# Splitting the second group's router logits load at row 126, as the first group's already is

## The chip, the cores and the metric

The kernel runs on one core of one Trainium2 chip. The metric is the device time of one execution, in microseconds (us); for a kernel that is timed it is the median of several runs. A profile is one more execution, recorded by the hardware profiler; its span runs from its first instruction to its last.

## The reference: top-2 gating and a scaled copy

There are 16 x 1024 = 16384 tokens. Each has 512 floats of `x` and 8 router logits. The output holds each token's 512 floats twice, each copy scaled by one of two weights:

```python
probs = softmax(router_logits)                     # over 8 experts
topk_indices = np.argsort(probs, axis=-1)[..., -2:]
topk_probs = np.take_along_axis(probs, topk_indices, axis=-1)
topk_probs = topk_probs / np.sum(topk_probs, axis=-1, keepdims=True)
out = (x[:, :, None, :].repeat(2, axis=2) * topk_probs[..., None])
```

Normalised over the two best experts, the softmax is a sigmoid of the difference of the two largest logits, so the kernel needs only that difference. The input is 33.6 MB of `x` and 0.5 MB of logits, the output 67.1 MB, in float32 throughout.

## The kernel before, in words

The 128 partitions of SBUF hold tokens. `GROUPS = [65, 63]` (line 42) cuts the tokens into two groups: in the first each partition holds 65 consecutive tokens, in the second 63. So one partition's logits are a run of 65 x 8 x 4 = 2080 bytes of memory for the first group and of 63 x 8 x 4 = 2016 bytes for the second. These runs are called rows below; a transfer of logits moves up to 128 of them, one for each partition.

All loads and all stores but one are issued by SyncE (SP), in program order; the first store is issued by ScalarE (ACT). `keep_in_program_order` holds the order as written, so SP's list is fixed: a load of 2 tokens and one of 4 tokens for each partition (line 122), then the logits (the `if` at line 128), then loads of 28 and 31 tokens, which ends the first group's input. The logits come in three transfers: the first group's rows 0 to 125, its rows 126 and 127 (both line 133), and the second group's 128 rows in one (line 136). Behind them stand the first group's stores (line 156), each waiting for VectorE, then the second group's three loads (16, 16 and 31 tokens), which wait until the first group's buffers have been stored, then the second group's stores. An `x` load of 28 tokens moves 28 x 2048 = 57344 bytes for each partition, one of 31 tokens 63488; a store of 15 tokens moves 61440 (two copies of each token), one of 16 tokens 65536. At the very end an empty SP instruction (line 160) waits for all but the last transfer.

`top2_weights` (line 14) takes all logits of both groups at once: VectorE (DVE) finds the largest and second largest of 8 by a tree of max and min over both groups' 128 tokens for each partition. Its first instruction (line 26) therefore waits for all logits transfers. Line 36 takes the difference, ACT makes the two weights (lines 37 and 38). Then DVE multiplies (line 143): `x` rows times the two weights, into the buffer `osp` or in place into `xs`, and each product is stored. The logits lie in `osp` too, in a part of it that later products overwrite.

The framework gives every transfer one of eight completion semaphores, in turn. A transfer that is given a semaphore which an earlier transfer has used waits, where it isn't already known to be done, until that earlier one has landed.

Of the kernel before, what the change touches and what calls it, by code (L numbers as in the profile page):

```python
# [1 line left out]

# [4 lines left out]

F32 = mybir.dt.float32
ALU = mybir.AluOpType
ACTF = mybir.ActivationFunctionType  # L10
P = 128


def top2_weights(nc, WA, dlt, room, logits, E):

    tt = nc.vector.tensor_tensor
    hi, lo, n = None, None, E  # L20
    while n > 1:
        n //= 2
        if hi is None:
            a, b = logits[:, :, 0:n], logits[:, :, n : 2 * n]
            nhi, nlo = room(n), b
            tt(nhi, a, b, op=ALU.max)  # L26
            tt(nlo, a, b, op=ALU.min)  # L27
        else:
            a, b = hi[:, :, 0:n], hi[:, :, n : 2 * n]
            nhi, nlo, tmp = room(n), room(n), room(n)  # L30
            tt(tmp, lo[:, :, 0:n], lo[:, :, n : 2 * n], op=ALU.max)  # L31
            tt(nlo, a, b, op=ALU.min)  # L32
            tt(nlo, nlo, tmp, op=ALU.max)  # L33
            tt(nhi, a, b, op=ALU.max)  # L34
        hi, lo = nhi, nlo
    tt(dlt, hi[:, :, 0], lo[:, :, 0], op=ALU.subtract)  # L36
    nc.scalar.activation(WA[:, :, 0], dlt, ACTF.Sigmoid, scale=-1.0)  # L37
    return nc.scalar.activation(WA[:, :, 1], dlt, ACTF.Sigmoid, scale=1.0)  # L38

GROUPS = [65, 63]

LOADS = [[2, 4, 28, 31], [16, 16, 31]]
BASE = [0, 1]

STORES = [
    [(0, 3, "osp", 0), (3, 15, "osp", 3), (18, 16, "xs", 0), (34, 15, "osp", 0), (49, 16, "xs", 33)],
    [(0, 16, "osp", 2), (16, 16, "xs", 0), (32, 15, "osp", 0), (47, 16, "xs", 32)],
]  # L50

L = 18

FREE = [3, 2]


@with_exitstack
def kernel(
    ctx: ExitStack,
    tc: tile.TileContext,  # L60
    x: bass.AP,
    router_logits: bass.AP,
    k: bass.AP,
    out: bass.AP,
):
    nc = tc.nc
    B, S, D = x.shape
    E = router_logits.shape[-1]
    N = B * S
    assert int(k) == 2 and E == 8 and N == P * sum(GROUPS)  # L70
    M = N // P

    x_v, o_v, rl_v = [], [], []
    t0 = 0
    for n in GROUPS:
        t1 = t0 + P * n
        x_v.append(
            x.rearrange("b s d -> (b s) d")[t0:t1].rearrange("(p m) d -> p m d", p=P)
        )
        o_v.append(  # L80
            out.rearrange("b s k d -> (b s) k d")[t0:t1].rearrange(
                "(p m) k d -> p m k d", p=P
            )
        )
        rl_v.append(
            router_logits.rearrange("b s e -> (b s) e")[t0:t1].rearrange(
                "(p m) e -> p m e", p=P
            )
        )
        t0 = t1  # L90

    wpool = ctx.enter_context(tc.tile_pool(name="wpool", bufs=1))
    xs = wpool.tile([P, max(GROUPS), D], F32)
    osp = wpool.tile([P, L, 2, D], F32)
    WA = wpool.tile([P, M, 2], F32)
    dlt = wpool.tile([P, M], F32)


    flat = osp.rearrange("p l k d -> p (l k d)")
    taken = [0]  # L100

    def room(n):
        o = taken[0]
        taken[0] += M * n
        return flat[:, o : o + M * n].rearrange("p (m n) -> p m n", n=n)

    logits = room(E)

    def place(where, at, n):

        if where == "osp":
            return osp[:, at : at + n]
        return xs[:, at : at + 2 * n, :].rearrange("p (r k) d -> p r k d", k=2)

    moved = []
    m0 = 0
    for g, G in enumerate(GROUPS):
        x0, r = BASE[g], 0
        for n in LOADS[g]:
            moved.append(  # L120
                tc.keep_in_program_order(
                    nc.sync.dma_start(  # L122
                        xs[:, x0 + r : x0 + r + n, :], x_v[g][:, r : r + n, :]
                    )
                )
            )
            r += n
            if g == 0 and r == 6:
                n0 = GROUPS[0]
                for p0, p1 in [(0, 126), (126, P)]:  # L130
                    moved.append(
                        tc.keep_in_program_order(
                            nc.sync.dma_start(logits[p0:p1, :n0], rl_v[0][p0:p1])  # L133
                        )
                    )
                tc.keep_in_program_order(nc.sync.dma_start(logits[:, n0:], rl_v[1]))  # L136
                weights = top2_weights(nc, WA, dlt, room, logits, E)
        assert r == G
        for r, n, where, at in STORES[g]:
            og = place(where, at, n)  # L140
            again = where == "osp" and at == 0 and r > 0
            for a, b in [(0, FREE[g]), (FREE[g], n)] if again else [(0, n)]:
                product = nc.vector.tensor_tensor(  # L143
                    og[:, a:b],
                    xs[:, x0 + r + a : x0 + r + b, :]
                    .unsqueeze(2)
                    .to_broadcast([P, b - a, 2, D]),
                    WA[:, m0 + r + a : m0 + r + b, :]
                    .unsqueeze(3)
                    .to_broadcast([P, b - a, 2, D]),  # L150
                    op=ALU.mult,
                )

            queue = nc.scalar if g == r == 0 else nc.sync
            moved.append(
                tc.keep_in_program_order(queue.dma_start(o_v[g][:, r : r + n], og))  # L156
            )
        m0 += G

    seen = tc.keep_in_program_order(nc.sync.nop())  # L160
    for ins in [weights, product] + moved[:-1]:
        tc.add_manual_dep(
            seen.ins,
            ins.ins.name,
            mybir.DependencyInfo(
                mybir.DependencyClass.Sync, mybir.DependencyReason.DATA
            ),
            reason="all but the last transfer is done",
        )


# [1 line left out]
_INS = ['x', 'router_logits', 'k']  # L173
_OUTS = [((16, 1024, 2, 512), 'float32')]

_NUMBERS = {'k': 2}


# [26 lines left out]
```

## Time and profile before

| | |
|---|---|
| time, median of 3 runs (lowest to highest) | 239.89 us (239.77 to 240.0) |
| the profiled execution's own time | 239.86 us |
| its span | 238.1 us |
| DVE busy | 141.9 us, 22 instructions |
| ACT busy | 1.8 us, 3 instructions |
| data moved by the DMA engines | 101.19 MB in 2592 packets |
| HBM read, written | 34.08 MB, 67.11 MB |

The core has 16 DMA engines. A transfer issued by SP (queue q1 in the profile) or by ACT (queue q10) is cut into packets that the engines work off, each engine in order. A view of a stretch of time counts a packet, its bytes and its time in full where the packet starts, so the DMA share of a short stretch can be over 1.00 or far below it; over a long stretch 1.00 means that 16 engines were busy all the time. "us to landing" is the time from the issue of a transfer to its completion.

### The profile page before, as it was taken

To read this page: it belongs to the slowest core of one execution; us is meant where nothing else is said; L and a number is where in the kernel's file an instruction comes from. 1 tells how busy PE (TensorE), PEld (TensorE's weight loads), DVE (VectorE), ACT (ScalarE), POOL (GpSimd) and SP (SyncE) were. 2 spreads that over 40 slices of the span, in tenths; PEclk is the share of its full clock that TensorE was granted. 3 is DMA by queue.
4 is the path that set the end of the run, shared out by engine and by line. 5 is a ranking of instruction groups with operands and counts; after the bars stand their busy time and mean duration, and the time that the engine had idled before them with its cause. 6 is when DMAs were issued, how large, how long until landed. Compare 5 with 4: busy or idle time off the path is not lost.

```text
span 238.1 us, 109 instructions
## 1 busy us (share of the span) xinstructions
DVE 141.9 (60%) x22; ACT 1.8 (1%) x3; POOL 0.2 (0%) x4
## 2 busy tenths in 40 slices
DVE  0560499999789999200000699999406999960000
ACT  2000000000000000000000000000000000000000
POOL 0000000000000000000000000000000000000000
DMA  7999998989898989989899999998998989989894
GB/s 261 419 443 503 406 461 381 465 372 495 363 496 374 507 351 475 495 352 529 352 435 424 418 479 448 405 507 363 440 440 363 518 352 507 454 372 518 352 518 187
DMA packets 2592, 101.19 MB, mean 425 GB/s; under 512 B 288, under 2 KB 416, under 8 KB 672
## 3 DMA queue, kind: packets, MB, share of 16 engines
q1 hardware_dynamic: 2448, 99.62, 97.3%
q10 hardware_dynamic: 144, 1.57, 1.6%
HBM read 34.08 MB, written 67.11 MB: 425 GB/s over the span
## 4 chain that ended last, share of the span: by engine, by line
DMA 48%; DVE 40%; SPq 1%; issue 0%; DVEq 0%
DVE osp L143 25%; DMA xs<-in_x_dram 25%; DMA out_dram<-osp 22%; DVE xs L143 14%; SPq L122 0%; SPq L133 0%; SPq L136 0%; SPq L156 0%; DVEq L143 0%
## 5 line engine op out<-in xcount | busy, mean ns | idle before, releaser
L143 DVE TENSOR_TENSOR osp<-xs,WA 128x3072 f32<-128x3072 f32 (+5 forms) x7 | 69.4, 9909 | 61.0 <-DMA xs<-in_x_dram 46.8
L143 DVE TENSOR_TENSOR xs<-xs,WA 128x16384 f32<-128x16384 f32 x4 | 68.9, 17225 | 0.1
L26 DVE TENSOR_TENSOR osp<-osp 128x512 f32<-128x512 f32 x1 | 0.7, 692 | 8.8 <-DMA osp<-in_router_logits_dram 8.8
L37 ACT ACT_TABLE_LOAD x1 | 1.3, 1283 | 0.7 <-PEq L186 0.7
L27 DVE TENSOR_TENSOR osp<-osp 128x512 f32<-128x512 f32 x1 | 0.7, 691 | 0.0
L32 DVE TENSOR_TENSOR osp<-osp 128x256 f32<-128x256 f32 (+1 forms) x2 | 0.7, 352 | 0.0
L34 DVE TENSOR_TENSOR osp<-osp 128x256 f32<-128x256 f32 (+1 forms) x2 | 0.7, 352 | 0.0
L31 DVE TENSOR_TENSOR osp<-osp 128x256 f32<-128x256 f32 (+1 forms) x2 | 0.7, 351 | 0.0
L33 DVE TENSOR_TENSOR osp<-osp 128x256 f32<-128x256 f32 (+1 forms) x2 | 0.7, 350 | 0.0
L37 ACT ACTIVATE WA<-dlt 128x128 f32<-128x128 f32 x1 | 0.3, 315 | 10.7 <-DVE dlt L36 10.7
L36 DVE TENSOR_TENSOR dlt<-osp 128x128 f32<-128x128 f32 x1 | 0.3, 293 | 0.0
L38 ACT ACTIVATE WA<-dlt 128x128 f32<-128x128 f32 x1 | 0.3, 298 | 0.0
L186 POOL MEMSET const-bfloat16-1.0<- 128x1 bf16 x1 | 0.1, 101 | 0.0
L186 POOL MEMSET const-uint8-127<- 128x1 uint8 x1 | 0.1, 101 | 0.0
L186 POOL MEMSET const-float32-0.0<- 128x1 f32 x1 | 0.1, 98 | 0.2 <-issue 0.2
L186 POOL MEMSET const-float32-1.0<- 128x1 f32 x1 | 0.1, 98 | 0.0
## 6 DMA issues: line engine op xcount, KB each, us to landing
out_dram<-osp SPq DMA_DIRECT2D x3, 7680.0 KB, 23.1
xs<-in_x_dram SPq DMA_DIRECT2D x2, 7936.0 KB, 41.4
xs<-in_x_dram SPq DMA_DIRECT2D x2, 4096.0 KB, 40.2
xs<-in_x_dram SPq DMA_DIRECT2D x1, 7168.0 KB, 24.2
out_dram<-osp ACTq DMA_DIRECT2D x1, 1536.0 KB, 26.5
xs<-in_x_dram SPq DMA_DIRECT2D x1, 1024.0 KB, 5.9
xs<-in_x_dram SPq DMA_DIRECT2D x1, 512.0 KB, 3.6
osp<-in_router_logits_dram SPq DMA_DIRECT2D x1, 255.9 KB
```

The lines of the kernel that those rows point to most:

```text
L26: tt(nhi, a, b, op=ALU.max)
L27: tt(nlo, a, b, op=ALU.min)
L31: tt(tmp, lo[:, :, 0:n], lo[:, :, n : 2 * n], op=ALU.max)
L32: tt(nlo, a, b, op=ALU.min)
L33: tt(nlo, nlo, tmp, op=ALU.max)
L34: tt(nhi, a, b, op=ALU.max)
L36: tt(dlt, hi[:, :, 0], lo[:, :, 0], op=ALU.subtract)
L37: nc.scalar.activation(WA[:, :, 0], dlt, ACTF.Sigmoid, scale=-1.0)
L38: return nc.scalar.activation(WA[:, :, 1], dlt, ACTF.Sigmoid, scale=1.0)
L143: product = nc.vector.tensor_tensor(og[:, a:b], xs[:, x0 + r + a : x0 + r + b, :] .unsqueeze(2) .to_broadcast([P, b - a, 2, D]), WA[:, m0 ...
L186: nc = _bacc.Bacc("TRN2", target_bir_lowering=False, num_devices=1)
```

## The change

The second group's logits are loaded in two transfers as well, rows 0 to 125 and rows 126 and 127, by the same loop as the first group's. SP issues four logits transfers instead of three, in the same place. Both parts of the second group are now in the list `moved`, which the last SP instruction waits for. The bytes, the rows, their places in memory and in SBUF and every instruction of DVE and ACT stay as they were.

```diff
             if g == 0 and r == 6:
-                n0 = GROUPS[0]
-                for p0, p1 in [(0, 126), (126, P)]:
-                    moved.append(
-                        tc.keep_in_program_order(
-                            nc.sync.dma_start(logits[p0:p1, :n0], rl_v[0][p0:p1])
+                at = 0
+                for h, m in enumerate(GROUPS):
+                    for p0, p1 in [(0, 126), (126, P)]:
+                        moved.append(
+                            tc.keep_in_program_order(
+                                nc.sync.dma_start(
+                                    logits[p0:p1, at : at + m], rl_v[h][p0:p1]
+                                )
+                            )
                         )
-                    )
-                tc.keep_in_program_order(nc.sync.dma_start(logits[:, n0:], rl_v[1]))
+                    at += m
                 weights = top2_weights(nc, WA, dlt, room, logits, E)
```

In the built program one more thing moves: with one transfer more ahead of them, all later transfers get the next of the eight semaphores. The load of 31 tokens of the first group so comes to the semaphore of the very first load (2 tokens), and SP waits for that load's landing before it issues the 31 tokens. No other transfer's waits change but in the semaphores' numbers; DVE's first instruction and ACT's store name four logits transfers instead of three.

## The prediction

> **What bounds the kernel now.** First the page: busy times and DMA queues.
>
> ```profile
> DVE 141.9 (60%) x22; ACT 1.8 (1%) x3; POOL 0.2 (0%) x4
> ...
> DMA packets 2592, 101.19 MB, mean 425 GB/s; under 512 B 288, under 2 KB 416, under 8 KB 672
> ...
> q1 hardware_dynamic: 2448, 99.62, 97.3%
> q10 hardware_dynamic: 144, 1.57, 1.6%
> ```
>
> DVE works 60% of the span; the packets of the two queues fill 97.3 + 1.6 = 98.9% of the 16 engines' time. So the next view cuts the span by stretches: until the logits are in, and from there to the last packets (columns: stretch, length, DVE, ACT, POOL, clock, DMA share, GB/s).
>
> ```profile
> 1.70:9.40 7.70, 0.61 (x1) 0.30 (x1) 0.00 (x0) 1.00 1.08 392
> 9.40:236.30 226.90, 141.31 (x22) 0.51 (x2) 0.00 (x0) 1.00 1.00 433
> ```
>
> From 9.40 to 236.30 us the share is 1.00 at 433 GB/s: no engine ever runs dry there. The time is therefore the number of bytes that an engine must move, plus the start, plus what slows packets down. Compute is off the path. The start and the end, by counts of packets in short stretches: 233.9 to 234.4, 234.4 to 234.7, 236.3 to 236.8, 236.9 to 237.0.
>
> ```profile
> DMA packets 15, 0.98 MB, mean 1966 GB/s; under 512 B 0, under 2 KB 0, under 8 KB 0
> ...
> q1 hardware_dynamic: 15, 0.98, 453.4%
> ```
> ```profile
> DMA packets 1, 0.07 MB, mean 218 GB/s; under 512 B 0, under 2 KB 0, under 8 KB 0
> ```
> ```profile
> DMA packets 15, 0.00 MB, mean 0 GB/s; under 512 B 15, under 2 KB 15, under 8 KB 15
> ```
> ```profile
> DMA packets 1, 0.00 MB, mean 0 GB/s; under 512 B 1, under 2 KB 1, under 8 KB 1
> ```
>
> The last set of big packets is one for each engine: 15 start before 234.4, one after it. Each lasts 4.534 x 16 x 0.5 / 15 = 2.42 us for 65536 bytes, 27.1 GB/s. Each engine closes a transfer with a tiny packet: 15 before 236.8, one after 236.9. So **one engine ends last, by 0.1 us at least**, and whatever is added to its packets is added to the time. The page's 288 tiny packets show how the split works already: 19 transfers (7 loads of `x`, 3 of logits, 9 stores) on 16 engines each would leave 304; 16 fewer is what results when the 126 rows use 14 engines (9 rows each, 2 packets fewer) and the 2 rows use two engines (14 fewer).
>
> **The change part by part.**
>
> (1) *Rows by engine, the term that counts.* 128 rows on 16 engines are 8 each. Split, 14 engines carry 9 rows of 2016 bytes, two of all engines one more, and two carry none. What does one row cost? Counts of 5.88 to 6.61 us, then 6.61 to 7.65, the two stretches in which logits move:
>
> ```profile
> DMA packets 123, 0.26 MB, mean 354 GB/s; under 512 B 16, under 2 KB 24, under 8 KB 117
> ...
> q1 hardware_dynamic: 123, 0.26, 90.4%
> ```
> ```profile
> DMA packets 142, 0.36 MB, mean 349 GB/s; under 512 B 18, under 2 KB 105, under 8 KB 140
> ...
> q1 hardware_dynamic: 142, 0.36, 130.5%
> ```
>
> First stretch: 0.904 x 16 x 0.73 = 10.56 us of packet time; off come 6 packets of 8 KB (8192 bytes at 27 GB/s, 0.30 us each, 1.8) and 16 tiny ones (about 0.01 each, 0.15); 8.6 us remain for 101 rows, 0.085 us a row. Second stretch: 1.305 x 16 x 1.04 = 21.7 us; off come two big packets (57344 bytes at 27.1 GB/s, 2.1 us each at least, 4.2) and 18 tiny ones (0.2); 17.3 us for 122 rows, 0.14 us a row. So rows go at full speed first and at little over half of it from 6.61 us on: **a slow stretch** costing 122 x (0.14 - 0.085) / 16 = 0.4 us for each engine. One row more is 0.085 to 0.14 us; I take 0.11, the middle, since with the split the row ends in either stretch. For the two engines with two rows more it is 0.22, and for the two without rows 8 x 0.085 to 8 x 0.14 = 0.7 to 1.1 less. The engine that ends last is one of the 14 by 14 in 16, and of the two with 0.22 by 2 in 16. Taken: **+0.11**; bounds 0 (if the slow stretch is a limit on all rows together, spreading the same rows otherwise costs nothing) and 2 x 0.14 = +0.28.
>
> [...]
>
> (2) *One more issue on SP.* Issue times, and the queue's order:
>
> ```profile
> L133 SPq DMA_DIRECT2D osp<-in_router_logits_dram x2: 242/350/457, 1.6 to 2.1; - x2
> ```
> ```profile
> 0.72 0.85 SPq L122 DMA_DIRECT2D xs<-in_x_dram  x2
> 1.63 0.74 SPq L133 DMA_DIRECT2D osp<-in_router_logits_dram  x2
> 2.41 0.36 SPq L136 DMA_DIRECT2D osp<-in_router_logits_dram  x1
> 2.81 0.95 SPq L122 DMA_DIRECT2D xs<-in_x_dram  x2
> 8.79 0.69 DVE L26 TENSOR_TENSOR osp<-osp 128x512 f32<-128x512 f32 x1 [8.79 <-DMA osp<-in_router_logits_dram]
> ...
> 16.65 0.37 ACTq L156 DMA_DIRECT2D out_dram<-osp  x1
> ...
> 43.26 0.35 SPq L156 DMA_DIRECT2D out_dram<-osp  x1
> ```
>
> 0.46 + 0.24 instead of 0.36: the 28 tokens are issued 0.34 us later, at 3.15 instead of 2.81. The first load was issued at 0.72, and the first packets start at 1.7 (below), a lag of 1.0; so the 28 tokens are ready at about 4.2. Who asks first for them shows in the counts of 7.0 to 7.3 us:
>
> ```profile
> DMA packets 39, 0.18 MB, mean 584 GB/s; under 512 B 7, under 2 KB 35, under 8 KB 37
> ```
>
> 39 - 37 = 2 big packets, the only two up to 7.65: the two engines without first-group rows, at 7.0 at the earliest. Without their 8 second-group rows too they ask at 5.9 to 6.3. Cover 1.7 us: cost 0; without cover, 0.34.
>
> (3) *The new wait on SP.* The 31 tokens wait for the landing of the first load (512 KB). Behind it on SP stand the first group's stores, the first issued at 43.26.
>
> ```profile
> DMA  0000000000000000099991532679998989997977
> ...
> xs<-in_x_dram SPq DMA_DIRECT2D x1, 7168.0 KB, 24.2
> ...
> xs<-in_x_dram SPq DMA_DIRECT2D x1, 512.0 KB, 3.6
> ```
>
> (The first line is 0 to 4 us in slices of 0.1.) The first load lands at 0.72 to 1.10 + 3.6 = 4.3 to 4.7; the 31 tokens are issued then instead of by 3.76, and needed only when the 28 tokens run out, at about 2.81 + 24.2 = 27. Cover over 20 us: cost 0.
>
> (4) *The weights come later.* DVE's line 26 starts with the last logits landing, 8.79; two engines with two more rows put it off by up to 0.28, ACT's store from 16.65 to 16.9 and the first SP store from 43.26 to 43.5. With the lag of 1.0 that is ready at 44.5. Counts of 44 to 47 us and of 47.0 to 47.2:
>
> ```profile
> DMA packets 16, 1.02 MB, mean 339 GB/s; under 512 B 0, under 2 KB 0, under 8 KB 0
> ```
> ```profile
> DMA packets 4, 0.12 MB, mean 614 GB/s; under 512 B 2, under 2 KB 2, under 8 KB 2
> ```
>
> Up to 47 all engines move the last 63488 bytes of the 31 tokens; the first two turn to the store after 47.0. Cover 2.5 us: cost 0; if a store came later than that, each 1 us late is 1 us. Later stores give no stall either, by the share of 1.00. The two engines with no rows come up to 1.1 us earlier: cover 1.4 still.
>
> (5) *The end.* The last SP instruction names more transfers, all long landed: 0.
>
> **Sum:** 239.86 (the profiled execution) + 0.11 = 239.97. The runs' median, 239.89, is 0.03 above that execution, so the sum stands for either.
>
> [...]
>
> **The rivals.**
>
> *A: the slow stretch goes.* For: rows of the first group, in 14 engines' shares, ran at 0.085 while the second group's, in 16 shares, met the slow stretch. Against: 35 of the first group's rows stand in the slow stretch too (140 under 8 KB - 105 under 2 KB). If it goes: 239.97 - 0.4 = 239.57.
>
> *B: the last engine catches up.* Starts of the last packets but one of the second group's 31 tokens, and of the first ones of the store behind them:
>
> ```profile
> 155.30:155.50 0.20, 0.20 (x1) 0.00 (x0) 0.00 (x0) 1.00 1.46 635
> 155.50:155.94 0.44, 0.44 (x1) 0.00 (x0) 0.00 (x0) 1.00 4.33 1876
> 155.94:156.00 0.06, 0.06 (x1) 0.00 (x0) 0.00 (x0) 1.00 2.44 1058
> 160.30:160.70 0.40, 0.40 (x1) 0.00 (x0) 0.00 (x0) 1.00 5.69 2458
> 160.70:160.90 0.20, 0.20 (x1) 0.00 (x0) 0.00 (x0) 1.00 0.00 0
> 160.90:160.95 0.05, 0.05 (x1) 0.00 (x0) 0.00 (x0) 1.00 3.03 1311
> ```
>
> 2, 13 and 1 packets at 155.3 to 156.0 without a straggler; at 160 us 15 start by 160.7, one after 160.9. The lag of 0.2 that sets the end arose where loads turn to stores. With other engines ahead it may fall otherwise: 239.97 - 0.2 = 239.77. With A: 239.37.
>
> *C: the slow stretch spreads (slower).* Place: 5.9 to 8 us. The 14 engines have 18 small rows each in a line instead of 17. If all go at 0.14, that is 18 x 0.055 = 1.0 us lost instead of 0.4, so +0.6 on top of 0.11: 240.57. It decides once over two thirds of the rows are slow: 12 x 0.055 = 0.66, 0.26 more than now, with 0.22 for an engine of two more rows is 0.48. For: the engines without rows start their 28 tokens beside the others' rows sooner, and the slow stretch began when two engines were ahead. Against: those two read big packets only from 7.0, 0.4 after it began.
>
> *D: the new 2-row transfer makes its engines stop.* If they took up the next transfer only after one lag of 1.0, the two end at 239.97 + 1.0 = 240.97. Against: the first group's 2 rows stand in the same line, and rows flowed at a share of 0.90 and more. [...]
>
> **How the numbers follow.** Forecast 239.97 (239.86 to 240.14): 0.54. A alone 0.13, B alone 0.12, A with B 0.06; C 0.12; D 0.03. 0.2% is 0.48 us, about what a measurement of this kernel can tell from no change. Faster than 239.41: A with B, 0.06, and a little of A, 0.02: 0.08. Slower than 240.37: C for the most, 0.11, and D, 0.03: 0.14. Same: 0.78. The range from 239.45 to 240.4 leaves out A with B, D and nearly all of C, 0.2.
>
> **What would show it.** 288 packets under 512 B again (20 transfers, 32 fewer than 320) and 416 under 2 KB; SP's logits issues 1.4 to 1.5 us in all; line 26 at 8.8 to 9.1 us; two engines at big packets from about 6 us; a share of 1.00 from 9.4 us to the end. A slow stretch of other length shows as other time for the rows between 6 and 8 us (A, C), a last tiny packet closer to the rest as B. I'm wrong if a stretch after 9.4 us is below 1.00, or if small rows move over 0.48 us.

## The result, and the profile after

| | before | changed |
|---|---|---|
| median time, 12 runs each | 239.94 us (239.77 to 240.12) | 240.47 us (240.28 to 240.98) |
| ratio to before, 95% interval | | 1.0023 (1.0014 to 1.0032) |
| the profiled execution: time, span | 239.86, 238.1 us | 240.28, 238.5 us |

The changed kernel is slower by 0.53 us, where 0.11 was forecast; the time lies 0.07 above the range. The profiled executions are 0.42 apart.

The page of the changed kernel has the same packets, and one line that moved by a whole microsecond:

```profile
DMA packets 2592, 101.19 MB, mean 424 GB/s; under 512 B 288, under 2 KB 416, under 8 KB 672
...
L26 DVE TENSOR_TENSOR osp<-osp 128x512 f32<-128x512 f32 x1 | 0.7, 691 | 9.8 <-DMA osp<-in_router_logits_dram 9.8
```

DVE's first instruction waits for the logits until 9.8 us instead of 8.8. Its SP queue and that instruction, in order of time:

```profile
1.63 1.44 SPq L134 DMA_DIRECT2D osp<-in_router_logits_dram  x4
3.11 1.63 SPq L122 DMA_DIRECT2D xs<-in_x_dram  x2
9.83 0.69 DVE L26 TENSOR_TENSOR osp<-osp 128x512 f32<-128x512 f32 x1 [9.83 <-DMA osp<-in_router_logits_dram]
```

From the end of the first loads to the start of the 28 tokens on all engines (5.8 to 9.3 us), first the kernel before, then the changed one:

```profile
DMA packets 330, 1.52 MB, mean 435 GB/s; under 512 B 48, under 2 KB 176, under 8 KB 304
...
q1 hardware_dynamic: 330, 1.52, 119.4%
```
```profile
DMA packets 334, 1.56 MB, mean 445 GB/s; under 512 B 48, under 2 KB 176, under 8 KB 304
...
q1 hardware_dynamic: 334, 1.56, 139.9%
```

Both stretches hold the same work but for four 8 KB packets: 48 tiny packets, 128 rows of 2016 and 128 of 2080 bytes, 16 big packets (the first 57344 bytes of the 28 tokens, one for each engine), and 10 or 14 packets of 8 KB. At full speed (0.009, 0.082, 0.085, 2.116 and 0.305 us; the kernel with neither group split, below, shows that these prices add up exactly) that is 58.7 and 60.0 us of packet time. The engines took 1.194 x 16 x 3.5 = 66.9 and 1.399 x 56 = 78.3. So the **excess** is 8.2 / 16 = 0.51 us for each engine before, and 18.3 / 16 = 1.15 after. The same sum is made for each experiment below; it is the number to watch. The slow stretch of the prediction more than doubled, and it took in the big packets. The two engines without rows show that. Packets from 6.2 to 6.6 us of the changed kernel, then from 9.4 to 9.9:

```profile
DMA packets 74, 0.25 MB, mean 614 GB/s; under 512 B 9, under 2 KB 9, under 8 KB 72
```
```profile
DMA packets 2, 0.11 MB, mean 229 GB/s; under 512 B 0, under 2 KB 0, under 8 KB 0
```

74 - 72 = 2 big packets start by 6.6; these engines' second ones start only after 9.4: the packets started at 6.28 and 6.46 took 3.2 and 3.3 us instead of 2.1. Before, where they started at 7.0 to 7.3, the two second ones came between 9.4 and 9.7:

```profile
DMA packets 2, 0.11 MB, mean 382 GB/s; under 512 B 0, under 2 KB 0, under 8 KB 0
```

So the lead of 0.4 us or more was lost at once.

Not all of 0.64 us more excess reached the end. The last 57344-byte packets of the 28 tokens, before (22.5 to 24.0 us) and changed (22.5 to 25.0):

```profile
q1 hardware_dynamic: 16, 0.92, 155.6%
```
```profile
q1 hardware_dynamic: 16, 0.92, 84.6%
```

1.556 x 16 x 1.5 / 16 = 2.33 us each before, 0.846 x 2.5 = 2.12 each in the changed kernel. So before lost 0.21 us there that the changed kernel didn't lose: 0.64 - 0.21 = 0.43, and the profiled times differ by 0.42. That the two meet so closely is partly chance: the last packets of the 31 tokens took 0.06 us more in the kernel before as well (0.800 x 3.0 = 2.40 from 44 to 47 us, against 0.976 x 2.4 = 2.34 from 44 to 46.4), 14 engines of the changed kernel carry a row more (0.08 at full speed), and a mean over 16 engines isn't the engine that ends last. At the end (tiny packets from 236.0 to 236.1 and from 236.8 to 237.4 of the changed kernel) the two light engines are done 0.7 us and more ahead of the other 14:

```profile
DMA packets 2, 0.00 MB, mean 0 GB/s; under 512 B 2, under 2 KB 2, under 8 KB 2
```
```profile
DMA packets 14, 0.00 MB, mean 0 GB/s; under 512 B 14, under 2 KB 14, under 8 KB 14
```

### The profile page after: what moved, and what is told of

Same layout as the page of the kernel before. It is cut to its first block, busy times and chain, and to the rows that moved or that the text cites. A ratio compares the mean times of both kernels' runs of the same rounds, so it can differ in the third digit from the quotient of the medians.

```text
span 238.5 us, 111 instructions
## 1 busy us (share of the span) xinstructions
DVE 141.9 (60%) x22; ACT 1.8 (1%) x3; POOL 0.2 (0%) x4
## 4 chain that ended last, share of the span: by engine, by line
DMA 48%; DVE 40%; SPq 1%; issue 0%; DVEq 0%
DMA xs<-in_x_dram 25%; DVE osp L146 25%; DMA out_dram<-osp 22%; DVE xs L146 14%; SPq L134 1%; SPq L122 0%; SPq L159 0%; DVEq L146 0%
## 5 line engine op out<-in xcount | busy, mean ns | idle before, releaser
L146 DVE TENSOR_TENSOR osp<-xs,WA 128x3072 f32<-128x3072 f32 (+5 forms) x7 | 69.4, 9909 | 60.4 <-DMA xs<-in_x_dram 46.4
## 6 DMA issues: line engine op xcount, KB each, us to landing
out_dram<-osp SPq DMA_DIRECT2D x3, 7680.0 KB, 22.9
```

Of the source, the lines that this page charges most:

```text
L146: product = nc.vector.tensor_tensor(og[:, a:b], xs[:, x0 + r + a : x0 + r + b, :] .unsqueeze(2) .to_broadcast([P, b - a, 2, D]), WA[:, m0 ...
```

## The experiments

All kernels start from the changed one. Most have its inner loop over a table of cuts, one list for each group:

```diff
+CUTS = [[(0, 126), (126, P)], [(0, 126), (126, P)]]     # the changed kernel
-                    for p0, p1 in [(0, 126), (126, P)]:
+                    for p0, p1 in CUTS[h]:
```

Excess, by the sum above, and line 26 of each profiled execution; times are medians, ratios against the kernel before on the same chip:

| kernel | logits transfers | excess, us | line 26 at | median | ratio (95%) |
|---|---|---|---|---|---|
| before | 126+2, 128 | 0.51 | 8.8 | 239.94 | 1 |
| changed | 126+2, 126+2 | 1.15 | 9.8 | 240.47 | 1.0023 (1.0014 to 1.0032) |
| e1_none | 128, 128 | 0.00 | 8.3 | 239.91 | 1.0001 (0.9992 to 1.0009) |
| e2_second_only | 128, 126+2 | 0.50 | 9.0 | 240.03 | 1.0006 (0.9997 to 1.0014) |
| e3_even | 126+2, 112+16 | 1.31 | 9.9 | 240.17 | 1.0010 (1.000 to 1.002) |
| e4_after_x6 | 126+2, 126+2, no wait | 1.04 | 9.8 | 240.21 | 1.0015 (1.0006 to 1.0024) |
| e5_after_again | 126+2, 126+2 | 1.41 | 10.3 | 240.89 | 1.0033 (1.0021 to 1.0045) |
| e6_split_and_tokens | 126+2, tokens 32+31 | 0.7 | 9.2 | 239.92 | 0.9999 (0.999 to 1.0007) |
| e7_tokens | 128, tokens 32+31 | 0.0 to 0.1 | 8.5 | 240.18 | 1.0015 (1.0001 to 1.0029) |
| e8_halves | 128, 64+64 | 0.85 | 9.7 | 239.99 | 0.9997 (0.9986 to 1.0008) |

**First set: shares, or one more transfer?** Theory S put the loss down to the uneven shares, theory W to the fourth transfer and its wait. e1 to e3 change the table of cuts (to one cut `(0, P)`, and to `[(0, 112), (112, P)]` for the second group in e3); e4 keeps it and changes the loads:

```diff
-LOADS = [[2, 4, 28, 31], [16, 16, 31]]
+LOADS = [[6, 28, 31], [16, 16, 31]]
```

Expected of e1_none:

> Neither group is split: two logits transfers of 128 rows, 8 rows of each group on each of the 16 engines. The kernel before stands at 239.94 us, the changed one at 240.47. Theory S (shares): what costs is that 14 engines carry 9 rows and the two others run ahead; then no split is at or below the kernel before, 239.5 to 239.95, with the last tiny packets within 0.6 us. Theory W (one more transfer): what costs is the fourth logits transfer, its issue and the wait that it gives to the 31 tokens; then with two transfers the time is that of before within 0.15, 239.8 to 240.1.

239.91 us, which fits both theories. But its stretch from 5.8 to 9.3 us is a find (the first line is the rate in 40 slices of 0.09 us; big packets, counted where they start, make the high numbers from the 18th on):

```profile
GB/s 468 374 398 95 354 286 380 404 428 428 402 377 396 393 393 392 415 2289 369 3484 4002 46 1311 0 0 0 0 0 0 0 0 0 0 0 0 0 0 0 0 0
DMA packets 335, 1.56 MB, mean 447 GB/s; under 512 B 48, under 2 KB 176, under 8 KB 304
...
q1 hardware_dynamic: 335, 1.56, 107.7%
```

1.077 x 56 = 60.3 us of packet time for 48 tiny packets (0.4), 256 rows (21.4), 16 big ones (33.9) and 15 of 8 KB (4.6): that is full speed, to the last 0.1. From the 8th slice on its rows flow at about 400 GB/s until the last ones. The changed kernel's, in the same slices, sink to half of that from the 13th on, as the single big packets in between (817 and the like) stand out:

```profile
GB/s 468 422 282 330 284 941 309 1012 380 356 308 282 259 233 210 209 278 207 230 230 161 184 817 138 138 2081 207 1380 748 2012 701 678 655 655 0 0 0 0 0 0
```

**With neither group split there is no slow stretch.** So the slow stretch of the kernel before was itself made by the first group's split.

> The second group is split at 126, the first isn't: three logits transfers as before, and no wait for the 31 tokens. Theory S: the second group's 14 shares alone bring a good part of the loss, 240.1 to 240.5, with two engines ahead at the 28 tokens. Theory W: three transfers as before, so 239.8 to 240.1.

240.03, just below what S asked and inside W's. Its excess, 0.50, is that of the kernel before: for the sum it doesn't matter which group is split.

> The second group is split at row 112 in place of 126: 112 rows are 7 on each of 16 engines, 16 rows one on each, so each engine has 8 rows as before, in two transfers. Four logits transfers and the wait for the first load stay as in the changed kernel. Theory S: as the kernel before, 239.8 to 240.1. Theory W: as the changed kernel, 240.3 to 240.7.

240.17, between the two, with line 26 as late as in the changed kernel and an excess even larger (the profiled execution, at 240.98, was the slowest of its eleven runs):

```profile
DMA packets 356, 1.61 MB, mean 459 GB/s; under 512 B 64, under 2 KB 192, under 8 KB 320
...
q1 hardware_dynamic: 356, 1.61, 148.0%
```

1.480 x 56 = 82.9 us against 62.0 at full speed (20 packets of 8 KB, 64 tiny): 1.31 for each engine. The second group's rows are even here and the first group's are cut at 126 as in the kernel before, so by number each engine has what it had there, with an excess of 0.51 (the 64 tiny packets are 16 for the load of 4 tokens, 16 for the first group and 16 for each of the second group's transfers, so both use all 16 engines). Uneven shares are not what slows rows; e8_halves below, with both groups even, says so again.

> The changed kernel with its first two loads (2 and 4 tokens) made one of 6, so that the 31 tokens get a semaphore that nothing has used and don't wait; the four logits transfers and their shares stay. Theory S: as the changed kernel, 240.3 to 240.7. Theory W: 239.8 to 240.1 if the wait is what costs, up to 240.3 if the issue is.

240.21, below S's band and inside W's wider one, in which the issue costs. The excess stays at 1.04 without any wait on SP. Shares and wait fall as accounts of the slow stretch: it grows with shares as they were before, and it comes without the wait. The further transfer and its issue are left for the next set.

**Second set: places, or number of transfers?** A transfer that is cut in another way hands its rows to the engines in another way: 126 and 2 rows leave 16 tiny packets together, one transfer of 128 as many (48 in the stretch of the changed kernel and of the kernel before, with 16 for the load of 4 tokens). With the two engines that run ahead of 14 in the trace above, that fits 9 of the 126 rows for an engine and 8 of the 128. Theory P says that engines then write to places in SBUF that other engines write to as well; which places an engine writes to is the author's assumption, no view shows it. Theory T says that each further transfer costs, however cut. The cuts get token bounds (or rows 0 to 63 and 64 to 127):

```diff
-                    for p0, p1 in [(0, 126), (126, P)]:
+                    for p0, p1, c0, c1 in CUTS[h]:
...
-                                    logits[p0:p1, at : at + m], rl_v[h][p0:p1]
+                                    logits[p0:p1, at + c0 : at + c1],
+                                    rl_v[h][p0:p1, c0:c1],
```

> The changed kernel again, written with a table of cuts, as the yardstick of this set. It stood at 240.47 us against 239.94 before, a ratio of 1.0023; both theories expect 240.3 to 240.6 here, line 26 at about 9.8 us and the last row of logits ending at about 8.7 us. Theory P (places): a transfer whose rows are handed to the engines in another way than those of 128 rows in one, so that several engines write into the same part of SBUF at once, is what slows rows and the packets beside them. Theory T (transfers): every further logits transfer between the first loads and the 28 tokens costs about 0.5 us there, however its rows are shared.

240.89, above the band, with an excess of 1.41 where the same program had 1.15: the stretch varies by some tenths from one execution to another.

> As the changed kernel, but the second group's two transfers are cut by tokens: all 128 rows with tokens 0 to 31, then all 128 with tokens 32 to 62. Four logits transfers, the wait for the first load and one more issue stay; each engine has the partitions that it has in a transfer of 128 rows. Theory P: only the first group's split is left, so as the kernel before, 239.8 to 240.1, line 26 at 8.8 to 9.1. Theory T: as the changed kernel, 240.3 to 240.6, line 26 at 9.7 to 10.

239.92, as P has it, and 0.97 below the changed kernel on the same chip, with the same number of transfers, the same wait and as long an issue. Line 26 is at 9.2, a little later than P's band, 0.6 earlier than in the first trace of the changed kernel and 1.0 earlier than in e5's. The sum over 5.8 to 9.3 us:

```profile
q1 hardware_dynamic: 479, 1.56, 129.7%
```

1.297 x 56 = 72.6 us against 61.5 (the full-speed sum of e7_tokens, below, which has the same packets): 0.7 for each engine, somewhat more than the 0.51 of the first group's cut alone in the kernel before, and half of e5's. **The fourth transfer, its issue and its wait cost nothing that shows in the time.**

> The first group in one transfer of 128 rows, the second in two cut by tokens: three logits transfers, none of which is cut by rows. Theory P: no slow stretch, rows at about 0.05 to 0.09 us as where neither group was split, the 28 tokens' packets begin within 0.6 us of each other, line 26 at 8.3 to 8.6, time 239.7 to 240.0. Theory T: as the kernel before, a slow stretch of about 0.4 us for each engine, line 26 at 8.8 to 9.0, 239.8 to 240.1; line 26 and the rows tell them apart, the time hardly.

> The first group in one transfer, the second in two halves by rows, 0 to 63 and 64 to 127: three logits transfers, each engine with 8 rows of each group in all, 4 and 4. Beside the kernel cut by tokens only the direction of the cut differs. Theory P: the halves hand the rows to the engines otherwise than 128 rows in one, so rows are slow, 0.12 us or more in the mean of the second group, and line 26 is 0.4 us or more later than with the cut by tokens. Theory T: as with the cut by tokens within 0.15 us.

These two differ only in the direction of the cut. Tokens first, then halves by rows, 5.8 to 9.3 us, each with its wait of line 26:

```profile
q1 hardware_dynamic: 479, 1.56, 110.1%
```
```profile
DVE osp L26 <- DMA osp<-in_router_logits_dram: 8.5, 1, 8.5
```
```profile
q1 hardware_dynamic: 356, 1.61, 135.0%
```
```profile
DVE osp L26 <- DMA osp<-in_router_logits_dram: 9.7, 1, 9.7
```

With 128 rows in each transfer 1.101 x 56 = 61.7 us; at full speed 60.4 if a half row took half a row's time, 61.5 at the 0.045 and 0.046 us that every half row in this trace took: hardly any excess. By halves 75.6 against 62.0, 0.85 for each engine, and line 26 is 1.1 us later. P is right on both counts, T wrong. In time P's band for e7 (239.7 to 240.0) was missed: 240.18, with runs from 239.65 to 241.5, and e8 at 239.99 isn't slower than before. An excess below about 0.9 hasn't been seen in the time.

**Third set: places in SBUF, or places in memory?** Two added transfers read the same 64 rows of memory again and write them, once to partitions 0 to 63, once to 32 to 95; neither group is split. The kernels differ in two numbers:

```diff
+                for o in (9216, 10240):
+                    moved.append(
+                        tc.keep_in_program_order(
+                            nc.sync.dma_start(
+                                flat[0:64, o : o + 504].rearrange(    # or flat[32:96, ...]
+                                    "p (m n) -> p m n", n=E
+                                ),
+                                rl_v[1][0:64],
+                            )
+                        )
+                    )
```

> Neither group is split (two logits transfers of 128 rows); behind them two added transfers read the second group's rows 0 to 63 once more and put them into an unused part of the buffer, partitions 0 to 63. This and the next kernel differ in nothing but the partitions that the added rows are written to. Theory P (places in SBUF): partitions 0 to 63 make the engines write over one another, so the added 128 rows are slow, 0.13 to 0.17 us each, and the 28 tokens' first packets start 0.4 us or more later than with partitions 32 to 95. Theory M (places in memory, or the way in which 64 rows are handed out): as with partitions 32 to 95 within 0.1 us.

> As the kernel that puts the added rows into partitions 0 to 63, but into partitions 32 to 95: the same memory is read in the same shares of 4 rows for each engine. Theory P: partitions 32 to 95 leave each engine a place of its own, so rows run at 0.08 to 0.09 us as where neither group is split, and the time is 0.2 to 0.6 us below that of partitions 0 to 63. Theory M: as with partitions 0 to 63, slow rows in both or in neither.

The stretch from 5.8 to 9.3 us, first partitions 0 to 63, then 32 to 95:

```profile
DMA packets 488, 1.69 MB, mean 482 GB/s; under 512 B 76, under 2 KB 326, under 8 KB 454
...
q1 hardware_dynamic: 488, 1.69, 153.7%
```
```profile
DMA packets 497, 1.84 MB, mean 526 GB/s; under 512 B 80, under 2 KB 336, under 8 KB 464
...
q1 hardware_dynamic: 497, 1.84, 128.0%
```

Partitions 32 to 95: 1.280 x 56 = 71.7 us; 80 tiny packets (0.7), 256 rows of 2016 (21.0), 128 of 2080 (10.9), 17 of 8 KB (5.2) and 16 big ones (33.9) make 71.7. Full speed, excess 0.0. Partitions 0 to 63: 153.7% is 86.1 us against 66.0 at full speed (250 rows of 2016, 13 big packets, 21 of 8 KB), 1.25 for each engine with the rest still to come. By the packets of the two traces the 128 added rows take 0.143 us each in the mean against 0.082, and the 28 tokens' first packets start at 7.8 to 10.0 us against 8.0 to 8.5: P had all of these later; the earliest isn't, most are. SP's issues are alike; line 26 is not:

```profile
2.57 1.30 SPq L143 DMA_DIRECT2D osp<-in_router_logits_dram  x2
3.92 1.30 SPq L122 DMA_DIRECT2D xs<-in_x_dram  x2
9.81 0.69 DVE L26 TENSOR_TENSOR osp<-osp 128x512 f32<-128x512 f32 x1 [9.81 <-DMA osp<-in_router_logits_dram]
```
```profile
2.57 1.35 SPq L143 DMA_DIRECT2D osp<-in_router_logits_dram  x2
3.96 1.15 SPq L122 DMA_DIRECT2D xs<-in_x_dram  x2
8.41 0.69 DVE L26 TENSOR_TENSOR osp<-osp 128x512 f32<-128x512 f32 x1 [8.41 <-DMA osp<-in_router_logits_dram]
```

Line 26 doesn't wait for the added transfers, yet it starts 1.40 us later beside those into partitions 0 to 63: the jam holds up the landing of the logits, too. The times are 241.19 (1.0052, 1.0035 to 1.0069) and 240.53 (1.0035, 1.0014 to 1.0056), 0.66 apart, a little over P's band; both kernels move 0.26 MB more than the kernel before. The intervals overlap, and the profiled execution of the first, at 242.66 us, was the slowest of its five runs, so the time says less than the rows do. The memory that is read, the rows and the transfers are the same, so **it is the place in SBUF that decides** whether these rows are slow (0.143 us a row, or 0.082). That the cut at row 126 is slow for the same reason is inferred: no run wrote its rows to other partitions, and no view names the engine or the place of a packet. What sets partitions 0 to 63 (excess 1.25 us) apart from 32 to 95 (0.0) no run shows.

**Fourth set: why does the first group's split cost nothing?** e1_none has no excess and the kernel before 0.51, but their times are equal. Something takes the lead away. Theory G blamed ACT's store, which runs beside the loads from 20 us on; theory F said that loads lose it by themselves. The store goes to SP, behind the loads:

```diff
-            queue = nc.scalar if g == r == 0 else nc.sync
+            queue = nc.sync
```

> Neither group split, and the first store is issued by SP behind the loads in place of ACT, so that no store runs beside the first group's loads. Theory G: ACT's store beside the loads is what takes the lead of 0.35 us away again at 17 to 25 us; then no 57344-byte packet is slower than 2.13 us, the lead stays, and the time is 0.2 to 0.5 us below that of the next kernel. Theory F: the loads lose it even without a store beside them; packets at 17 to 25 us are slow again and the time is that of the next kernel within 0.15 us.

> The kernel before with its first store on SP. Theory G: no loss at 22 to 25 us; 0.2 to 0.5 us above the kernel with neither group split and the store on SP, 0.5 to 0.8 below the changed kernel with the store on SP. Theory F: as the kernel with neither group split, 0.3 to 0.6 below the changed one.

> The changed kernel with its first store on SP; the 31 tokens then don't wait for the first load. Theory G: it had nothing to lose at 22 to 25 us before, so it stands against the kernel before with the store on SP by the whole delay of its rows, 0.5 to 0.8 us. Theory F: by 0.3 to 0.6 us, as with the store on ACT.

240.28, 239.96 and 240.92 (1.0014, 1.0000 and 1.0040 of before, with intervals 1.0006 to 1.0023, 0.9991 to 1.0008, 1.0025 to 1.0055). Both theories fall: without any split it is now 0.32 *slower* than with the first group's, and the changed kernel stands 0.96 above. Taking the store away from beside the loads doesn't take the loss away: it stands in another load. The last packet of the 31 tokens on each engine, e11_none_sp (40.6 to 41.4 us), then e12_before_sp (40.9 to 42.2):

```profile
q1 hardware_dynamic: 16, 1.02, 404.1%
```
```profile
q1 hardware_dynamic: 16, 1.02, 180.5%
```

4.041 x 0.8 = 3.23 us a packet against 1.805 x 1.3 = 2.35. In e1_none (store on ACT) the loss is in the last packets of the 28 tokens, 22.9 to 23.8 us:

```profile
q1 hardware_dynamic: 16, 0.92, 276.4%
```

2.764 x 0.9 = 2.49 against 2.12. In each case the kernel without a jam at the front loses on the last rows of a load: 0.37 us for each engine here, 0.88 in e11_none_sp, against jams of 0.51 in the kernel before and 0.65 in e12_before_sp (1.299 x 56 = 72.7 us against 62.3). Why those rows slow down no run here tells; it stays open.

These traces bear out the finding of the first two sets as well: from 5.8 to 9.3 us e11_none_sp has no excess (107.7%, with the packets of e1_none), and e13_after_sp has 1.16 (1.414 x 56 = 79.2 us against 60.6). Of all 15 traces (the two of the change among them), the eleven with a cut by rows or with rows written to partitions 0 to 63 have 0.50 us or more, the four others 0.0 to 0.1.

## Why the prediction was wrong, point by point

- *What bounds the kernel*: right. The engines are busy to the end (in the changed kernel too a share of 1.00 from 9.40 to 236.00 us), and some 0.4 us more packet time is 0.42 us more in the profiled time.
- *(1) Rows by engine*: **the step that failed.** "One row more is 0.085 to 0.14 us; I take 0.11" priced the row and let the slow stretch stand as it was, 0.4 (0.51 by the full sum, which also takes in the rows after 7.65 us and the big packets). The slow stretch wasn't a given: it was the price of the first group's split, and the second split brings its own. 0.51 became 1.15, and the medians moved by 0.53, over the upper bound of 0.28. How many rows an engine has, which the term was worked out from, is not what counts (e3_even has 1.31 us of excess, e8_halves 0.85). That two engines carry two rows more, behind the bound of 0.28, is an estimate that no run shows; what the trace of the changed kernel shows is two engines that turn to the 28 tokens at 6.28 and 6.46 us. The sign was in the rows quoted there, where packets of nearly the same size took 0.085 and then 0.14; the prediction asked what the stretch costs and not what makes it.
- The lead of the two engines without rows (0.7 to 1.1 "less") is real at 6.6 us and gone by 9.4, since their big packets are caught in the jam. At the end they are again 0.7 ahead, which helps nobody.
- *(2), (3), (5)*: right. The four issues take 1.44 us, SP waits 0.9 us for the first load before it issues the 31 tokens, the engines find their packets all the same; e6_split_and_tokens has all of this at 239.92.
- *(4) Later weights*: the delay is 1.04 us and not 0.28, but its cover held. The first packet of the first SP store starts between 46.4 and 46.8 us, and that store was issued at 43.99 and so, with the lag of 1.0, ready at 45.0.
- *Rival A* had the sign of the split wrong: e1_none shows the stretch gone without splits. *Rival B* didn't come: 14 engines end within 0.6 us. *Rival C* named the place (5.9 to 8 us) and nearly the time, 240.57, but its reason, more small rows in a line on 14 engines, is refuted by e3_even, whose engines have as many rows as in the kernel before, and by e8_halves, whose engines all have 8 of each group; that it came near the time is luck. *Rival D*, a stop of about 1 us on the two engines of the new 2-row transfer, isn't seen: all 14 engines with rows end within 0.6 us.

How much of an excess reaches the time stays partly open: in the first two sets kernels with 0 to 0.85 us lie between 239.91 and 240.18, those with more than 1 between 240.17 and 240.89, and the part that is lost again later isn't explained. Summed over all packets that start after 5.8 us, against the fastest packet of each size, the excess of the profiled executions is 0.8 to 0.95 us for each engine in e1_none, e2_second_only, e6_split_and_tokens, e7_tokens, e8_halves and the kernel before (239.86 to 240.18 us), and 1.3 to 1.8 in e4_after_x6, the changed kernel, e5_after_again and e3_even (240.27 to 240.98). So an early excess of up to 0.85 was made up for by smaller losses later, and a larger one wasn't.

## What to carry to other kernels

When a small transfer has to be cut, cut it along the free dimension and keep all 128 partitions in each part: each cut by rows that was tried here, at 126, 112 and 64, brought slow packets, and not only among the cut rows (0.50 to 1.41 us of excess for each engine), while the cut by tokens alone brought next to none (0.0 to 0.1). The places decide, as far as the added rows show it (0.0 us of excess on partitions 32 to 95, 1.25 on 0 to 63), so a transfer of fewer partitions isn't slow as such. When a trace shows packets of one size at two speeds, find out what makes the slow ones before pricing a change beside them. In this kernel, which is bound by transfers, a delay at the front wasn't worth its full size at the end (0.64 us more excess, 0.42 us more time), so take sums of packet time by stretch and look for the place where the rest comes back.

## What the runs showed of the hardware that wasn't expected

- Two transfers of 64 rows to partitions 0 to 63 bring a jam of 1.25 us and more for each engine; the same rows to partitions 32 to 95 go at full speed (71.7 us of packet time, as summed). So half of the partitions took these rows at full speed where that half was 32 to 95.
- Packets of 57344 bytes on the two engines without small rows took 3.2 and 3.3 us instead of 2.1 while the others' rows were jammed.
- Without splits, the last rows of a load are slow instead: 2.49 us instead of 2.12 in e1_none, 3.23 instead of 2.35 in e11_none_sp.
